# A causal convolution on one core: three row loads of the first loop blocks move into the set-up, and one of the block after them

## The chip, the cores and the metric

The kernel runs on one core of a Trainium2 chip. The metric is the device time of one execution in microseconds; the kernel before takes 733.92 us, the median of three runs (733.46 to 734.03). Lower is better.

## The reference

```python
def setup_inputs():
    B, S, D, K = 8, 4096, 512, 8
    return {
        "x": np.random.randn(B, S, D).astype(np.float32),
        "kernel": np.random.randn(K, D, D).astype(np.float32),
    }

def reference(x, kernel):
    B, S, D = x.shape
    K = kernel.shape[0]
    out = np.zeros_like(x)
    for k in range(K):
        if k == 0:
            shifted = x
        else:
            shifted = np.concatenate([np.zeros((B, k, D), dtype=np.float32), x[:, :-k, :]], axis=1)
        out += np.matmul(shifted, kernel[k])
    return out.astype(np.float32)
```

Each output row is the sum over eight taps `k` of the input row `k` steps earlier (zero before the start of a sequence) times the 512 x 512 matrix of that tap.

## The kernel before

**Layout.** The 8 x 4096 time steps are cut into 128 runs of 256 consecutive steps, one run to a partition. "Row t" is the set of the t-th steps of all 128 runs, a 128 x 512 matrix, so that one row is one matmul operand and the 256 rows are worked through in order. Because a run begins in the middle of a sequence, the rows -7 to -1 are the last rows of the run before, shifted by one partition.

**How a row reaches the matmuls.** The product needs rows with their 512 columns on the partitions, in bf16. From row 12 on this takes two transfers. `load_x(t)` (a DMA on POOL's queue, line 93) casts rows t to t+3 from float32 to bf16 and puts them into a scratch tile `xd` in DRAM; there are enough such tiles that no load waits for a free one. `transpose_x(t)` (a DMA transpose on SP's queue, line 100) then brings these four rows transposed into the ring `XR` of 20 row slots in SBUF, at slot (t + 4) mod 20; it waits for its load and for the last readers of the rows that it overwrites. The set-up also reads rows 0 to 11 directly, transposes them on PE, and loads the eight tap matrices on POOL's queue ahead of everything else.

**The arithmetic.** Rows 0 to 3 are computed by 32 direct products in the set-up. The other 252 rows go in 21 steps of 12 rows. A step saves matmuls by a fast-convolution scheme: it has four nodes, named `PL`, `MI`, `H1` and `H0`, and node k of the list `nodes` (four to a step, from 1) starts at row `n.t` = 4, 16, 28 and so on. Each node forms differences or sums of `XR` rows on DVE (`z`, then `s`, `A` and `F`, line 84), multiplies them by precombined weight matrices on PE (line 125), corrects partial results on DVE and ACT, and is brought out to tiles `y` of a five-buffer pool (`e0`, `e1`, lines 84, 87 and 247). A `PL` node of start t reads rows t-3 to t+7, as does `MI`; `H1` reads t-7 to t-1 and t+1 to t+7; `H0` reads t to t+3 and t+8 to t+11. So the `z` of node 13 (t = 40), for example, reads rows 37 to 47. A store (line 232, SP's queue) writes two output rows from a `y` tile, whose buffer is free again when the store has landed.

**The order.** All order is written by hand: the body is one sequence of calls, each engine takes its own instructions in that order, and each queue its own transfers. The set-up runs the direct products and most of the first step, with parts of the next. Then comes the loop of 21 blocks, called block 0 to block 20 here, over the list `ORDER` of tokens: token `name.i` in block m calls action `name` for node 4m + i + 1, unless `done` says that it was made already. The `AHEAD` table moves calls of the set-up to later nodes. In block 0 much of the list is done already.

**The loads in that order.** The set-up issues the loads of rows 12, 16, 20, 24, 28, 32 and 36 without a wait for compute (POOL reaches the last at 35.88 us). In the loop, actions `r0`, `r1`, `r2` of a node load rows `n.t + 36`, `+40` and `+44`, each made to wait for the DVE instruction that precedes it in the order (`behind`), so that it doesn't run ahead. A block's `ORDER` has three such tokens, `r1.6`, `r2.2` and `r0.2`; in block m they load rows 12m + 56, 12m + 48 and 12m + 40. They are skipped in block 0, and the table `LATE` makes up for it: row 40 is loaded at the end of block 0, and rows 44, 48 and 56 in block 1, beside the regular rows 68, 60 and 52 of that block. The transposes of a block are `x16`, `x20` and, at its end, `x12`: rows 32, 36 and 40 in block 1, rows 44, 48 and 52 in block 2. Rows 24 are transposed twice, in the set-up and in block 0.

POOL also adds pairs of half tiles for the middle output rows (`ga0` to `gb1`, line 276, four to a block from block 1 on). The first of them in each block, at 102.51, 134.78 and 173.38 us in blocks 1, 2 and 3, is used as the mark of the block.

Of the kernel before, what the change touches and what calls it, by code (L numbers as in the profile page):

```python
# [14 lines left out]
def kernel(  # L15
# [79 lines left out]
    def rows(o, t, n):  # L95
        return load(o, xr[:, t:t + n, :])
# [9 lines left out]
    def load_x(t):  # L106
        if t < RUN:
            xd[t] = dpool.tile([P, 4, D], bf, name="xd")
            return rows(xd[t], t, 4)
# [285 lines left out]
    done = set()  # L395

    def do(name, k):
        if k < len(nodes) and (name, k) not in done:
            done.add((name, k))
            ACTS[name](nodes[k])  # L400

    def go(k, name):
        do("a1" if name == "b1" else name, k + AHEAD.get(name, 0))
# [6 lines left out]
    for k in range(7):  # L410
# [184 lines left out]
    go(2, "F0")  # L595
    load_x(32)
    go(4, "l01")
    load_x(36)
    go(4, "l00")
    go(3, "s1")  # L600
    go(4, "b1")
# [10 lines left out]
    go(4, "z")  # L612
    go(4, "A")
    go(4, "g1")
    go(4, "s0")
    go(4, "v0")
    go(4, "d0")
# [2 lines left out]
    go(4, "a1")  # L620
    go(4, "d1")

    done |= {(name, k) for name in ("ga0", "gb0", "ga1", "gb1") for k in (1, 2, 3, 4)}
    done |= {(name, k) for name in ("F0", "F1", "dt", "v0", "v1", "d0", "d1") for k in LEAF}
    LATE = {(0, "d1.4"): [("wl", 8)], (0, "z.6"): [("wh", 8)], (0, "F1.5"): [("r0", 3)],
            (1, "F1.2"): [("r1", 3)], (1, "A.4"): [("r2", 3)], (1, "v1.4"): [("r1", 7)]}
    for m in range(NB):
        for token in ORDER:
            name, i = token.split(".")
            if m or name[0] != "r":  # L630
                do(name, 4 * m + int(i) + 1)
            for late in LATE.get((m, token), ()):
                do(*late)

# [29 lines left out]
```

## Time and profile before

| What | Value |
|---|---|
| median of 3 runs | 733.92 us (733.46 to 734.03) |
| the profiled execution, its own time | 735.01 us |
| its span, first to last instruction | 733.2 us |
| mean granted TensorE clock | 0.993 |
| POOL busy | 142.9 us (19%) |
| ACT busy | 277.3 us (38%) |
| share of the 16 DMA engines: transposes and stores on SP's and ACT's queue (q1) | 48.4% |
| share of the 16 DMA engines: loads on POOL's queue (q0) | 31.1% |
| loads into `xd` | 61 of 512 KB, 7.5 us from issue to landing (median) |
| transposes into `XR` | 62, 5.6 us from issue to landing (median) |
| stores | 127 of 512 KB, 3.5 us from issue to landing (median) |

The span of 733.2 us lies within the profiled execution's own time, with 1.8 us around it; that execution took 1.1 us longer than the median of the runs. Busy time of an engine is the time in which one of its instructions runs; the page also cuts the span into 40 slices of 18.3 us and gives each engine's busy share of every slice in tenths. A row of a timeline has the start, the time taken, the engine, the line, the operation, the tile written and the tiles read, and in brackets how long the engine stood idle just before and what ended that. A transfer has two such times: its issue on POOL's or SP's queue, which is what the timeline shows, and its landing, which the reader of a tile waits for.

### The profile page before, as it was taken

What the parts mean: (1) busy time and instruction counts of PE and PEld (TensorE: products, weight loads), DVE (VectorE), ACT (ScalarE), POOL (GpSimd) and SP (SyncE); (2) the same over time, 40 slices, a digit from 0 to 9 for tenths busy, and PEclk for the clock granted to TensorE, in tenths of its full rate; (3) what the DMA queues carried; (4) which work ended last, traced back from release to release, by engine and by line L of the source; (5) the groups of instructions that cost most, each with busy time, mean ns of one, the idle gap of its engine ahead of it and who ended that gap; (6) DMA issues with size and microseconds to landing.
All of it is one profiled execution on the core that took longest, in us unless ns stands there. A gap on an engine that the chain in (4) does not pass through costs nothing. (4 is left out here: it accounts for less than half of the span.)

```text
span 733.2 us, 8954 instructions
## 1 busy us (share of the span) xinstructions
PE 703.6 (96%) x3205; PEld 315.6 (43%) x3270; DVE 697.4 (95%) x767; ACT 277.3 (38%) x428; POOL 142.9 (19%) x160
## 2 busy tenths in 40 slices
PE   8979989899999999999999999999999999999996
PEld 4434434334444444444444444444444444444442
DVE  1989999799999999999999999999999999999995
ACT  3052433333425253343424335243433524334251
POOL 4200022121131202113121221312112030211202
PEclk9999999989999999999999999999999999999999
DMA  9994699968879796887969788796887979685324
GB/s 200 211 202 126 216 173 242 172 199 180 203 166 222 212 197 189 214 201 169 219 201 187 206 196 204 193 213 195 173 225 176 213 208 182 181 166 180 105 115 172
DMA packets 161451, 139.38 MB, mean 190 GB/s; under 512 B 132224, under 2 KB 136320, under 8 KB 161280
## 3 DMA queue, kind: packets, MB, share of 16 engines
q1 hardware_dynamic: 147536, 100.42, 48.4%
q0 software_dynamic: 13728, 38.15, 31.1%
q8 instruction: 25, 0.41, 0.2%
q10 hardware_dynamic: 144, 0.26, 0.1%
q14 instruction: 18, 0.15, 0.1%
HBM read 77.33 MB, written 99.09 MB: 241 GB/s over the span
## 5 line engine op out<-in xcount | busy, mean ns | idle before, releaser
L125 PE MATMUL pp<-w,F 128*128 128x512 bf16 x1283 | 313.9, 380 | 2.0 <-issue 0.2
L125 PE MATMUL pp<-w,Z 128*128 128x512 bf16 x942 | 232.6, 380 | 2.8 <-DVE Z L84 1.7
L125 PEld LDWEIGHTS <-F 128*128 128x128 bf16 x1312 | 128.5, 98 | 158.8 <-issue 6.7
L276 POOL TENSOR_TENSOR y<-y 128x512 f32<-128x512 f32 x80 | 100.9, 1272 | 429.1 <-DVE Z L84 306.2
L125 PE MATMUL pp<-w,S 128*128 128x512 bf16 x659 | 161.3, 380 | 11.8 <-ACT pp L202 6.6
L84 DVE TENSOR_TENSOR Z<-XR 128x2048 bf16<-128x2048 bf16 (+3 forms) x109 | 154.6, 1437 | 6.7 <-DMA XR<-xd 5.0
L125 PEld LDWEIGHTS <-Z 128*128 128x128 bf16 x960 | 92.4, 98 | 118.2 <-DVE Z L84 12.3
L186 ACT COPY pp<-pp 128x512 f32<-128x512 f32 x82 | 46.7, 570 | 226.6 <-PE pp L125 226.6
L84 DVE TENSOR_TENSOR S<-Z 128x2560 bf16<-128x2560 bf16 x81 | 120.1, 1483 | 0.2 <-remote 0.2
L84 DVE TENSOR_TENSOR F<-S 128x1024 bf16<-128x1024 bf16 x160 | 109.4, 686 | 1.1 <-PE pp L125 0.4
L125 PEld LDWEIGHTS <-S 128*128 128x128 bf16 x672 | 65.6, 98 | 95.0 <-issue 20.4
L204 ACT ACTIVATE pp<-pp 128x512 f32<-128x512 f32 (+1 forms) x84 | 49.1, 585 | 89.2 <-DVE y L87 47.2
L208 ACT COPY DT<-pp 128x512 f32<-128x512 f32 x82 | 48.5, 591 | 59.6 <-PE pp L125 59.6
L93 POOL DMA_DIRECT2D xd<-in_x_dram x61 | 32.4, 531 | 143.7 <-DVE F L84 61.4
L84 DVE TENSOR_TENSOR pp<-DT,pp 128x512 f32<-128x512 f32 x82 | 56.4, 688 | 2.2 <-PE pp L125 2.2
L87 DVE SCALAR_TENSOR_TENSOR pp<-pp,DT 128x512 f32<-128x512 f32 x82 | 56.8, 692 | 0.0
L84 DVE TENSOR_TENSOR Z<-Z 128x1024 bf16<-128x1024 bf16 x78 | 53.6, 687 | 0.6
L84 DVE TENSOR_TENSOR y<-pp,y 128x1024 f32<-128x1024 f32 x42 | 51.2, 1218 | 1.9 <-PE pp L125 1.4
L202 ACT COPY pp<-pp 128x512 f32<-128x512 f32 (+1 forms) x84 | 49.8, 593 | 5.5 <-PE pp L125 5.5
L87 DVE SCALAR_TENSOR_TENSOR y<-pp,y 128x1024 f32<-128x1024 f32 x42 | 51.2, 1218 | 0.3 <-PE pp L125 0.3
L87 DVE SCALAR_TENSOR_TENSOR y<-y,pp 128x1024 f32<-128x1024 f32 (+1 forms) x41 | 48.6, 1187 | 1.8 <-PE pp L125 1.6
L247 ACT COPY y<-pp 128x1024 f32<-128x1024 f32 x40 | 40.7, 1017 | 24.8 <-PE pp L125 23.5
(33 smaller groups left out, 214.3 us busy)
## 6 DMA issues: line engine op xcount, KB each, us to landing
out_dram<-y SPq DMA_DIRECT2D x127, 512.0 KB, 3.5
xd<-in_x_dram POOLq DMA_DIRECT2D x61, 512.0 KB, 7.5
w<-in_kernel_dram POOLq DMA_DIRECT2D x8, 512.0 KB, 15.8
w<-in_x_dram SPq DMA_DIRECT2D x1, 1024.0 KB, 4.9
w<-in_x_dram POOLq DMA_DIRECT2D x2, 512.0 KB, 13.6
XR<-xd SPq DMA_TRANSPOSE x62, 5.6
w<-in_x_dram POOLq DMA_DIRECT2D x2, 256.0 KB, 18.4
w<-in_x_dram POOLq DMA_DIRECT2D x1, 384.0 KB, 20.1
```

The lines of the kernel that those rows point to most:

```text
L84: last["dve"] = nc.vector.tensor_tensor(out=o, in0=a, in1=b, op=op)
L87: last["dve"] = nc.vector.scalar_tensor_tensor(out=o, in0=a, scalar=by, in1=b, op0=MUL, op1=op)
L93: return nc.gpsimd.dma_start(out=o, in_=src)
L125: nc.tensor.matmul(bank, lhsT=comp[:, c * P:(c + 1) * P], rhs=w[:, c, :], start=start and c == 0, stop=c == DC - 1, skip_group_check=True)
L186: nc.scalar.copy(out=n.q[:, 0], in_=n.q[:, 1])
L202: nc.scalar.copy(out=o, in_=q)
L204: nc.scalar.mul(out=o, in_=q, mul=-1.0)
L208: nc.scalar.copy(out=DT, in_=n.q[:, 0])
L247: nc.scalar.copy(out=cc[b_], in_=p)
L276: behind(nc.gpsimd.tensor_tensor(out=cc[b_][:, j], in0=cc[b_][:, j], in1=dd[b_][:, j], op=ADD))
```

## The change

The loads of rows 40, 44 and 48 are issued in the set-up right behind that of row 36, without a wait for compute. The load of row 56 (`r1` of node 7) is issued in the set-up behind `g1`, with its wait for the DVE instruction ahead of it. The entries for the four in `LATE` go. The loop no longer skips the load tokens in block 0: the ones of that block are marked as done, so block 0 issues no load and block 1 its three regular ones, rows 68, 60 and 52.

```diff
     go(2, "F0")
     load_x(32)
     go(4, "l01")
-    load_x(36)
+    for t in range(36, 52, 4):
+        load_x(t)
     go(4, "l00")
...
     go(4, "A")
     go(4, "g1")
+    do("r1", 7)
     go(4, "s0")
...
+    done |= {("r0", 3), ("r1", 3), ("r2", 3)}
     done |= {(name, k) for name in ("ga0", "gb0", "ga1", "gb1") for k in (1, 2, 3, 4)}
     done |= {(name, k) for name in ("F0", "F1", "dt", "v0", "v1", "d0", "d1") for k in LEAF}
-    LATE = {(0, "d1.4"): [("wl", 8)], (0, "z.6"): [("wh", 8)], (0, "F1.5"): [("r0", 3)],
-            (1, "F1.2"): [("r1", 3)], (1, "A.4"): [("r2", 3)], (1, "v1.4"): [("r1", 7)]}
+    LATE = {(0, "d1.4"): [("wl", 8)], (0, "z.6"): [("wh", 8)]}
     for m in range(NB):
         for token in ORDER:
             name, i = token.split(".")
-            if m or name[0] != "r":
-                do(name, 4 * m + int(i) + 1)
+            do(name, 4 * m + int(i) + 1)
```

The functions that it calls are unchanged.

## The prediction

> I write L40 for the load of rows 40 to 43 into DRAM scratch (tile `xd`) and T40 for the transpose of the same rows into the ring `XR`. All times are microseconds of the profiled execution; a median later block is one of those whose first POOL add starts at 173.38 or after.
>
> **What bounds the kernel now.** I read the engine totals first, then the slices, to see whether one engine binds everywhere.
>
> ```profile
> PE 703.6 (96%) x3205; PEld 315.6 (43%) x3270; DVE 697.4 (95%) x767; ACT 277.3 (38%) x428; POOL 142.9 (19%) x160
> ...
> DVE  1989999799999999999999999999999999999995
> ```
>
> PE and DVE are both full nearly throughout, so a transfer matters only where one of them stands still. Apart from the first slices, one DVE digit is low: the eighth, from 128 to 147. Windows as long as a block show what that stretch lost.
>
> ```profile
> 90.50:122.40 31.90, 29.38 (x132) 12.92 (x134) 31.26 (x35) 11.10 (x19) 8.73 (x11) 1.00 0.92 212
> 122.40:154.30 31.90, 26.85 (x113) 11.54 (x113) 25.72 (x28) 10.49 (x16) 5.57 (x5) 0.89 0.83 165
> 154.30:186.20 31.90, 31.44 (x145) 14.18 (x146) 31.21 (x36) 12.63 (x20) 5.37 (x6) 1.00 0.82 198
> 186.20:218.10 31.90, 31.39 (x143) 14.01 (x145) 31.78 (x37) 12.63 (x20) 6.70 (x9) 1.00 0.83 198
> ```
>
> The columns after the length are PE, PEld, DVE, ACT and POOL busy, then the granted clock. DVE has 25.72 where later blocks have 31.8, PE 26.85 for 31.4, and the clock falls to 0.89 there alone. The timeline of that stretch names the wait:
>
> ```profile
> 144.03 2.02 DVE L84 TENSOR_TENSOR Z<-XR 128x3584 bf16<-128x3584 bf16 x1 [5.05 <-DMA XR<-xd]
> ...
> 147.85 1.44 PE L125 MATMUL pp<-w,S 128*128 128x512 bf16 x3 [4.47 <-ACT pp L204]
> ...
> 153.95 1.22 DVE L87 SCALAR_TENSOR_TENSOR y<-y,pp 128x1024 f32<-128x1024 f32 x1 [0.96 <-PE pp L125]
> ...
> 155.69 2.02 DVE L84 TENSOR_TENSOR Z<-XR 128x3584 bf16<-128x3584 bf16 x1 [0.52 <-PE pp L125]
> ```
>
> DVE is ready at 144.03 - 5.05 = 138.98 for the `z` of node 13 (rows 37 to 47) and waits for T44. PE then runs dry for 4.47, and DVE waits for it in turn. The issuing queues show why T44 is late; first SP, then POOL:
>
> ```profile
> 126.80 16.87 SPq L100 DMA_TRANSPOSE XR<-xd  x3
> 147.42 16.30 SPq L232 DMA_DIRECT2D out_dram<-y  x6
> 164.26 10.07 SPq L100 DMA_TRANSPOSE XR<-xd  x3
> ```
>
> ```profile
> 112.71 0.54 POOL L93 DMA_DIRECT2D xd<-in_x_dram  x1 [2.54 <-DVE Z L84]
> 113.95 2.50 POOL L276 TENSOR_TENSOR y<-y 128x512 f32<-128x512 f32 x2 [0.70 <-issue]
> 119.48 1.05 POOL L93 DMA_DIRECT2D xd<-in_x_dram  x2 [3.03 <-DVE Z L84]
> 121.41 0.52 POOL L93 DMA_DIRECT2D xd<-in_x_dram  x1 [0.88 <-DVE pp L84]
> ```
>
> By program order these are L48, then L60 and L56, then L52. The last three are still moving when T40, T44 and T48 are issued from 126.80: the landings in the trace are 127.3, 131.2 and 134.6, T40's 137.4, T44's 143.8. In the next block only two loads (158.01 and 159.94) precede the trio at 164.26, and it is issued in 10.07 instead of 16.87.
>
> **The change, part by part.**
>
> (1) *L44, L48 and L56 leave block 1, L40 leaves block 0.* On POOL that is 4 issues of 0.54, all in POOL's idle time: nothing. On the DMA engines one load costs 2.62: from 40 to 52.5, with loads filling them, the POOL queue moved 2.50 MB of 0.524 MB loads, 4.77 loads in 12.5. Two loads fewer than before (L48 and L56) are in flight in the 8 ahead of T40, so its backlog shrinks by about 5. Block 1 keeps L68, L60 and L52, as every later block has three. So T44 should land as there: 9.4, 10.9, 10.7 and 9.3 after the first transpose of its trio is issued (trios at 164.26, 196.17, 229.01, 292.54), against 17.0 here. DVE wants it 138.98 - 126.80 = 12.2 after: 1.3 to 2.9 of slack, so the wait goes entirely. Two sums of what goes with it:
> - by gaps: 5.05 for `XR`, then 0.17, 0.96 and 0.52 while DVE waits for the slowed PE, and 0.48 at 114.30, where DVE waits for an output tile whose store shared the engines with L44 and L48: 7.18.
> - by block lengths: the first POOL add of blocks 1 to 3 starts at 102.51, 134.78, 173.38, that is 32.27 and 38.60. The block at the same place in the ring comes five later, 31.73 and 31.80. The excess is 0.54 + 6.80 = 7.34, and 0.06 in the block after: 7.40.
>
> I take 7.40; it contains the same gaps and what PE lost between them. What is late next once the wait is gone is DVE itself, 31.8 busy in a block of 31.8.
>
> (2) *L40, L44 and L48 go behind L36 in the set-up.* POOL's issues there wait for the landing of the load eight earlier, so they go out at about 36.9, 39.4 and 41.8, with nothing else on POOL until 85. They are queued on the POOL ring behind L36 and lengthen its busy time by 3 x 2.62 = 7.9. What lies beside it is T12, on SP's ring:
>
> ```profile
> q0 software_dynamic: 690, 2.50, 99.0%
> q1 hardware_dynamic: 484, 0.12, 7.2%
> ...
> 39.47 12.70 SPq L100 DMA_TRANSPOSE XR<-xd  x1
> 52.23 1.14 SPq L232 DMA_DIRECT2D out_dram<-y  x2
> 57.80 4.41 SPq L100 DMA_TRANSPOSE XR<-xd  x2
> ...
> 66.96 1.22 DVE L84 TENSOR_TENSOR Z<-XR 128x2048 bf16<-128x2048 bf16 x1
> ...
> 72.50 2.09 DVE L84 TENSOR_TENSOR Z<-XR 128x1536 bf16<-128x1536 bf16 x2
> ```
>
> While the loads run (first two rows, 40 to 52.5), a transpose gets 7.2% of the engines: 4 KB of a load go by for every 256 bytes. T12 takes 17.0 to land (56.4), and the two stores at 52.23 (57.6 and 58.8), T16 (62.5) and T20 (64.9) stand behind it on SP's ring. All five move back by up to 7.9, less what T12 gets done meanwhile; I take 7.4. Then T12 lands at 63.8 and is wanted at 66.96; the first store at 65.0, its buffer wanted by DVE at 70.23; T16 near 69.5, wanted at 72.50; T20 at 72.3 at the latest, wanted at 73.36 by the second half of the same `z`. The engines stood at 2% from 65 to 72.5, which is the room that this uses. Cost on the path: nothing, with slack of 1.1 to 3. The bounds of the unknown are the price of a load: 2.62 here, and at most 3.9, the spacing of the landings 127.3 and 131.2, where loads met stores and transposes. At 3.9 T20 is 11.7 late, 3.3 over its 8.4 of slack, and the gain is 4.1. I take 2.62, since that row has the same loads beside the same T12. Below nothing there is no room: no wait of DVE in the set-up has one of these loads behind it.
>
> (3) *L56 moves behind the `g1` of the set-up* (DVE, 84.49 to 85.7) and so is issued near 85.8, at POOL's 0.54, with the next POOL work at 102.51. Its 2.62 share the engines with two stores and the repeated T24 (87.89, landing 93.2, wanted by the `z` at 99.95). T24 has 6.8 of slack, the stores' buffers are wanted by ACT at 88.94 (store landed 88.3) and 97.37. In turn L40 no longer meets T32, which took 8.9 to land. Bounds 0 to 1.5: at worst the ACT copy is 2.6 late and PE, which stood 1.68 before 95.76 anyway, covers 1.1. I take 0, since L40 issued at 97.19 moved nothing before 100, so L56 should start near 88.3, as that store ends.
>
> Two rules of the Trainium skill were held against this. "SBUF — State Buffer" (SBUF: two separate sides) says that POOL's DMA descriptors starve while certain DVE operations hold the port they share, about 3.1 instead of 0.62. Here all 61 row loads were issued in 0.52 to 0.55, with DVE busy 95% of the span. By the rule three issues would be 7.4 longer together, which 18 of queued loads would hide, so the sum stays the same. "TensorE: Matmul & The Clock Gate" (Part 1: The HAM clock gate) says that an idle window of about 3.4 halves PE's clock; the 4.47 gap here agrees (clock 0.80 from 140 to 150). By it a shorter stall would cost its own length and no more.
>
> **Sum.** 0 - 7.40 + 0 + 0. Against the profiled execution, 735.01 with a span of 733.2, that gives 727.6 and a span of 725.8. The median of the runs, 733.92, is 1.1 below the profiled one; I take the difference off it: **726.5**.
>
> **Rivals.**
> - *A. The set-up gives part back.* T20 has only about 1 of slack. At 3.9 per load DVE stands 3.3 at the `z` wanting T16 and T20: 733.92 - 4.1 = 729.8. For it: DVE is full there, so any lateness counts. Against: the engines were free for 7.5 ahead of the `z`.
> - *B. Slower.* The same place, deeper: if the POOL ring holds T12 back so long that the lag passes 8.4 + 5.8 = 14.2 (4.7 per load), DVE waits 5.8, and the 1.65 of gaps behind a PE gap as at 147.85 makes 7.4, all of the gain. At 5.6 per load: lag 16.8, stall 8.4 + 1.65 = 10.1, 736.6. Against: the seven loads from L12 to L36 landed at a spacing of 2.5 to 2.7.
> - *C. The wait in block 1 stays in part.* If T44's lateness is due to the stores ahead and not the loads, only one load's worth, 2.6, goes: 2.45 of DVE's wait stay, PE's gap stays short of 4.47 and the 1.65 with it goes: 729.0. Against: later blocks have the same six stores and no wait.
> - *D. It does not do what it says:* the loads leave, T44 comes as late, only the 0.48 goes: 733.4.
>
> **How the numbers follow.** Forecast 0.75 (own range 725.6 to 727.4: 7.18 to 7.40 with the runs' spread of 0.6 and up to 0.8 of stall), A 0.10, B 0.06, C 0.06, D 0.03. The range goes down by the spread to 725.4 and up to A's end, 730.2, which leaves out B, D and a little more. A measurement of this kernel tells about 0.2%, 1.5, from no change: faster 0.91 (forecast, A, C), same 0.03 (D), slower 0.06 (B).
>
> **What would show it.** Step 1: no DVE wait for `XR` near 139, the trio from about 126 issued in 9 to 11, the granted clock 1.00 from 140 to 160, block lengths of 31.7 to 31.9. Step 2: T12 landing about 24 after its issue, loads landing until 63, T20 near 72, and DVE without a gap at 66.96, 70.23 and 72.50. Step 3: no new ACT or PE gap from 88 to 98. I am wrong if DVE waits for `XR` or for a store between 66 and 75, or still waits near 139.

## The result, and the profile after

| What | Before | After |
|---|---|---|
| median of 16 runs each | 733.69 us (728.82 to 735.99) | 728.48 us (727.42 to 730.61) |
| profiled execution, its own time | 735.01 us | 728.58 us |
| its span | 733.2 us | 726.8 us |
| granted clock | 0.993 | 0.997 |

The ratio is 0.9936, with a 95% interval of 0.9918 to 0.9955: faster, by 5.2 us (0.7%) between the medians. The ratios, here and below, are worked out from the fast runs alone and are not quotients of the medians; two slow executions are left out of them (740.88 us in experiment 3, and 928.25 us of the kernel before, beside experiments 6, 8 and 12), while the medians hold them. The spread is a result too: all but three of the 16 runs after lie between 728.2 and 728.8 us, those before over 7 us. The stretch that had stood out, in windows of a block (the columns are as before: PE, PEld, DVE, ACT and POOL busy, then the clock), of the changed kernel:

```profile
90.50:122.40 31.90, 29.77 (x135) 13.26 (x137) 31.74 (x35) 12.17 (x20) 6.59 (x7) 1.00 0.83 195
122.40:154.30 31.90, 31.49 (x144) 14.06 (x146) 31.77 (x35) 12.62 (x20) 6.68 (x8) 1.00 0.85 198
```

DVE has 31.77 where it had 25.72, and the clock stays at 1.00. On SP's queue the trio of transposes at the end of block 1 is as short as the later ones (9.66 for 16.87):

```profile
127.32 9.66 SPq L100 DMA_TRANSPOSE XR<-xd  x3
142.99 14.46 SPq L232 DMA_DIRECT2D out_dram<-y  x6
157.98 10.62 SPq L100 DMA_TRANSPOSE XR<-xd  x3
```

POOL, and then DVE, around it:

```profile
120.00 0.54 POOL L93 DMA_DIRECT2D xd<-in_x_dram  x1 [2.46 <-DVE Z L84]
121.93 0.52 POOL L93 DMA_DIRECT2D xd<-in_x_dram  x1 [1.39 <-DVE pp L84]
135.30 1.27 POOL L276 TENSOR_TENSOR y<-y 128x512 f32<-128x512 f32 x1 [12.86 <-DVE Z L84]
136.60 0.54 POOL L93 DMA_DIRECT2D xd<-in_x_dram  x1
```

```profile
138.02 1.48 DVE L84 TENSOR_TENSOR S<-Z 128x2560 bf16<-128x2560 bf16 x1
139.59 2.02 DVE L84 TENSOR_TENSOR Z<-XR 128x3584 bf16<-128x3584 bf16 x1
```

Two loads (L60, L52) precede the trio, T44 lands at 137.35, and the `z` of node 13 starts with no bracket: no wait. The load at 136.60 is L80, of the next block; it matters below. In the set-up, SP's queue shows what the moved loads cost:

```profile
39.97 20.46 SPq L100 DMA_TRANSPOSE XR<-xd  x1
60.50 1.20 SPq L232 DMA_DIRECT2D out_dram<-y  x2
61.81 7.25 SPq L100 DMA_TRANSPOSE XR<-xd  x2
```

T12 takes 20.46 to be issued instead of 12.70. It lands at 64.74, T16 at 69.66, T20 at 71.76; DVE wants them at 68.07, 73.60 and 74.47 and has no gap there.

### The profile page after: what moved, and what is told of

Same layout as the page of the kernel before. It is cut to its first block, busy times and chain, and to the rows that moved or that the text cites. A ratio compares the mean times of both kernels' runs of the same rounds, so it can differ in the third digit from the quotient of the medians.

```text
span 726.8 us, 8952 instructions
## 1 busy us (share of the span) xinstructions
PE 701.1 (96%) x3205; PEld 314.9 (43%) x3270; DVE 696.9 (96%) x767; ACT 277.3 (38%) x428; POOL 142.7 (20%) x160
```

## The experiments

All times are medians, beside the kernel before on the same chip (733.07 to 733.50). The places named are those of the listing.

**1. The kernel before, profiled again.** No edit.

> The kernel before, once more, for a second profile of it. Theory (the wait for the transposes of rows 40 and 44 at the end of block 1 is a race between transfers, so its length differs from run to run): times between 729 and 736 us, and the profile shows a DVE wait for XR near 139 us of another length than 5.05 us; the first weights land at 11.2 or at 12.3 us, whichever way that start fell. Rival (the wait is a fixed 5.05 us, and the spread of the times comes from elsewhere): the same wait within 0.3 us, whatever the time.

Median 733.28 us over 12 runs (728.18 to 735.05). The profiled one took 729.28 us, and its `z` of node 13 reads

```profile
140.30 2.02 DVE L84 TENSOR_TENSOR Z<-XR 128x3584 bf16<-128x3584 bf16 x1 [0.68 <-PE pp L125]
```

T44 landed at 140.10 (the bracket names PE, but DVE starts 0.2 after that landing), where the first profile had 143.84. The same program waits 0.68 us in one execution and 5.05 us in another. Blocks 1 and 2 took 33.09 and 32.31 us, 1.9 over the usual, not 7.4; most of the 1.9 is a wait of 1.30 at 114.93 for an output tile whose store was late (0.48 at 114.30 in the first profile). The two executions differ by 5.73 us in their times, and these two blocks (5.5) and the landing of the first weights (10.95 for 11.19) make up the whole of it. So the length of the wait is not fixed: the same transfers, issued in the same order, end in one way or the other. I call that a race.

**2. Load 56 alone moved; 3. load 56 alone left in block 1.**

```diff
# 2: the kernel before
     go(4, "g1")
+    do("r1", 7)
...
-            ..., (1, "v1.4"): [("r1", 7)]}
# 3: the changed kernel
-    do("r1", 7)
...
+            ..., (1, "v1.4"): [("r1", 7)]}
```

> The kernel before with the load of row 56 alone moved to the set-up; rows 40, 44 and 48 stay in the loop. Theory (every load that is queued in the 8 us ahead of the trio of transposes holds it up by its own 2.6 to 3.9 us): the DVE wait near 139 us shrinks from 5.05 to between 1.2 and 2.5 us, block 1 to block 2 takes 33 to 34.5 us, time 729.5 to 731 us. Rival (the stores ahead of the transposes are the cause): wait 4.5 to 5 us, time about 733.5 us.

> The changed kernel with the load of row 56 left in block 1 where it was; rows 40, 44 and 48 in the set-up. Theory: one load of 2.6 to 3.9 us more ahead of the trio than in the changed kernel, where row 44 landed 2.2 us ahead of DVE: a wait of 0.4 to 1.7 us comes back, time 729 to 730.5 us. Rival (the early loads of rows 40 to 48 did all of it): no wait, 728.5 us.

(2) 729.26 us, ratio 0.9940 (0.9925 to 0.9956): in its profile T44 lands at 138.71, and the `z` of node 13 has no wait:

```profile
140.03 2.03 DVE L84 TENSOR_TENSOR Z<-XR 128x3584 bf16<-128x3584 bf16 x1
```

What DVE waits for there is 0.27 for `XR` at 106.94, and 1.36 at 115.26 for a store that met L44 and T36 (landing at 112.11 and 113.76). (3) 733.36 us, ratio 0.9984 (0.9965 to 1.0003), no better than before, with

```profile
143.61 2.03 DVE L84 TENSOR_TENSOR Z<-XR 128x3584 bf16<-128x3584 bf16 x1 [5.00 <-DMA XR<-xd]
```

So it is L56 that counts: with it gone the wait is gone, with it back the whole wait is back, although L40, L44 and L48 have left the loop. L48 had landed at 120.24 in the kernel before, 6.6 us ahead of the trio; its leaving wins nothing at the `z`. Ahead of the trio stand L60, L56 and L52 in the kernel before and in (3), L60 and L52 in the changed kernel and in (2). Waits that add up load by load, as I had it, give 1.2 to 2.5 us in (2) and 0.4 to 1.7 in (3): both missed. One load makes the difference between no wait and 5 us, which is more than its own 2.6 to 3.9.

**4. A load that nobody reads.** The changed kernel, with rows loaded a second time at the place of L56.

```diff
+    def again(t):
+        behind(rows(dpool.tile([P, 4, D], bf, name="xd"), t, 4))
...
+            (1, "v1.4"): [("xx", 9)]}
```

> The changed kernel with one load of four rows made once more in block 1, at the place where the load of row 56 stood, into a scratch tile that nobody reads. Theory (traffic alone does it: one load more ahead of the trio is enough to lose the race against the load of row 80): as with row 56 left there, median about 733 us, spread 729 to 735. Rival (it is rows 40 to 56 themselves coming late, or POOL's order): no wait, 728.5 us.

733.88 us, ratio 1.0009 (0.9989 to 1.0029): the gain is gone. T44 landed at 143.34, and DVE waited:

```profile
143.53 2.03 DVE L84 TENSOR_TENSOR Z<-XR 128x3584 bf16<-128x3584 bf16 x1 [5.14 <-DMA XR<-xd]
```

Traffic alone does it; which rows come late is no matter.

**5. Load 80 held back.** The kernel before, with the first load of block 2 behind the `z` of node 13.

```diff
+            ..., (2, "v0.3"): [("r1", 15)]}
...
-            if m or name[0] != "r":
+            if (m or name[0] != "r") and (m, token) != (2, "r1.6"):
```

> The kernel before with one edit: in block 2 the load of row 80 is issued not right behind the first POOL add (136 us) but after the z of node 13, behind v0.3; rows 40 to 56 stay where they were. Theory (a race: the transposes of rows 40 and 44 come late by the loads ahead, and it is the load of row 80, whose 4 KB packets reach the engines at about 138.5 us, that holds up the last packets of row 44 until 143): the DVE wait near 139 us falls from 5 us to below 0.8 us in every run, time 728.5 to 730 us with a small spread. Rival (the loads ahead alone make the wait, as I predicted it): no change, 733 us with the spread of before.

729.16 us (727.55 to 730.84), ratio 0.9961 (0.9941 to 0.9982), with all of L40, L44, L48 and L56 where they were. The wait of its `z` is a little over the 0.8 that was expected at most:

```profile
139.17 2.02 DVE L84 TENSOR_TENSOR Z<-XR 128x3584 bf16<-128x3584 bf16 x1 [0.89 <-DMA XR<-xd]
```

The queues from 138.5 to 143 us in experiment 4, where L80 was issued at 135.49 (columns: packets, MB, share of the 16 engines; q1 is SP's, q0 POOL's):

```profile
q1 hardware_dynamic: 556, 0.14, 71.0%
q0 software_dynamic: 103, 0.36, 46.2%
```

and in this one, where L80 is issued at 142.48:

```profile
q1 hardware_dynamic: 1837, 0.46, 49.8%
```

Without L80 the transposes move 1837 packets in these 4.5 us, with it 556 (920 in the profile of experiment 1, where L80 is there too). In the kernel before, L80 is the second row of POOL in block 2:

```profile
134.78 1.27 POOL L276 TENSOR_TENSOR y<-y 128x512 f32<-128x512 f32 x1 [12.86 <-DVE Z L84]
136.08 0.54 POOL L93 DMA_DIRECT2D xd<-in_x_dram  x1
```

Its first packet moves at 138.6, 2.5 us after the issue; in experiment 4 at 137.7, in the changed kernel at 138.5. The reading is: if T44 is through by then (137.35 in the changed kernel), nothing happens; if much of it is left, the remainder is held up by L80 and lands with it: 143.84 and 143.93 in the kernel before, 143.34 and 143.23 in experiment 4. The line is not sharp: in experiment 1 L80's first packet moved at 138.6 too, and T44 landed 1.5 us later, at 140.10. The loads ahead decide whether the race is lost; L80 sets how much that costs.

**6. Both: the unread load, and load 80 held back.** The edits of 4 and 5 on the changed kernel.

> The changed kernel with the repeated load in block 1 (which took it back to 733.9 us) and, besides, the load of row 80 moved behind the z of node 13. Theory (the repeated load alone makes row 44 late by 0 to 1 us, and the load of row 80 makes 5 us of it): a wait below 1 us near 139 us, 728 to 729.5 us. Rival (the repeated load is what costs): 733 us as without the second edit.

729.15 us, ratio 0.9951 (0.9934 to 0.9968), against 733.88 without the second edit. The profiled wait was 2.44 us and not below 1, so the loads ahead alone can still cost that much; the median is in the range.

```profile
140.88 2.03 DVE L84 TENSOR_TENSOR Z<-XR 128x3584 bf16<-128x3584 bf16 x1 [2.44 <-DMA XR<-xd]
```

Set side by side, the profiles split the wait into its two parts. T44 lands after the first transpose of its trio is issued, by the number of loads issued in the 8 us ahead of that (DVE asks for it at about 12.2):

| Loads ahead | T44 lands after | Where |
|---|---|---|
| none, one | 7.5, 7.6 us | experiments 11, 10 |
| two | 10.0 to 11.0 us | the changed kernel, 2, 7, 8, 9, 12 |
| three, L80 held back | 12.9, 14.4 us | 5, 6 |
| three, L80 in its place | 12.7, and 17.0 to 17.1 us | 1, and before, 3, 4 |

The third load brings T44 over the limit by 0.5 to 2.2 us; L80 adds up to about 4 us more, or, as in experiment 1, nothing that shows.

**7. The three loads at 77 us, 8. at 62 us, 9. at 59 us.** The changed kernel, with the loads behind a DVE instruction.

```diff
# 7; in 8 and 9 they wait for a DVE instruction noted earlier, behind go(2, "s") or wsum(MI, LO, MID)
-    for t in range(36, 52, 4):
-        load_x(t)
+    load_x(36)
+    do("r0", 3)
+    do("r1", 3)
+    do("r2", 3)
```

> The changed kernel with the loads of rows 40, 44 and 48 not in the first stretch, where they hold up the transposes of rows 12 to 20, but behind the DVE instruction at about 77 us, where the DMA engines are half idle. Theory (the set-up hides those three loads in full): 728.5 us, within 0.5 us, with row 20 landed at about 65 to 66 us instead of 71.8. Rival (the three loads cost something in the set-up, which is why the time came out at 728.5 and not 726.5): 726.5 to 727.5 us.

> The changed kernel with the loads of rows 40, 44 and 48 made to wait for the DVE instruction at 62 us, so that they move between 65 and 73 us, where the DMA engines stood at 2% in the kernel before: behind the transposes of rows 12 to 20 and ahead of that of row 24. Theory (it is a question of which transfer on SP's queue they meet, and there they meet none): row 20 lands at 65 us, no DVE wait, the time of the changed kernel within 0.5 us. Rival (any later place than the first stretch costs, as 77 us did): 731 us and more.

> As the kernel with the three loads at 62 us, but waiting for the DVE instruction that ends at about 59 us, so that they are through before the store of 72.6 us and before the transpose of row 24. They share the engines with the transposes of rows 16 and 20: row 20 lands at 68 to 72 us, wanted at 73.4. Theory A (with nothing moved ahead of 55 us the first weights land at 11.0 to 11.2 us, as in all six profiles without loads added there, and no transfer is waited for): span 725.6 to 725.9, time 727.3 to 727.7 us, 1 us below the changed kernel. Theory B (the start varies by itself): median 728.3 to 728.7 us, as the changed kernel.

(7) 736.77 us, ratio 1.0045 (1.0028 to 1.0062): slower than before, against both guesses. SP's queue, then POOL's, then DVE in its profile:

```profile
77.77 9.28 SPq L100 DMA_TRANSPOSE XR<-xd  x1
87.15 3.05 SPq L232 DMA_DIRECT2D out_dram<-y  x3
98.88 12.25 SPq L100 DMA_TRANSPOSE XR<-xd  x4
```

```profile
77.61 1.55 POOL L93 DMA_DIRECT2D xd<-in_x_dram  x3 [41.32 <-DVE y L84]
```

```profile
106.54 1.23 DVE L84 TENSOR_TENSOR Z<-XR 128x2048 bf16<-128x2048 bf16 x1 [6.64 <-DMA XR<-xd]
```

T24, issued at 77.77, met these loads and L56 behind them and landed 21.1 us later; the second T24 waits for the first, T28 and T32 stand behind both on SP's queue, and DVE is out of rows for 6.64 us. (8) 728.42 us, ratio 0.9950 (0.9931 to 0.9968), as the changed kernel, though not quite without a wait: DVE stands 0.65 for a store that was issued at 72.6 and met the last load. (9) 729.97 us, ratio 0.9967 (0.9946 to 0.9988): four us earlier the loads meet T16 and T20. T20 lands at 74.58, and DVE waits 1.29 for it, and 1.30 for PE at 101.51. Neither theory of (9) held, since both had T20 in time. In these four places it is the transpose that the loads meet there, and its slack, that decides whether the place is free, and not how busy the DMA engines are on average.

**10. One load more in the first stretch, 11. three more.** `range(36, 52, 4)` becomes `range(36, 56, 4)` and `range(36, 64, 4)`; the loads go from where they stood.

> The changed kernel with the load of row 52 also issued in the set-up, right behind row 48: four loads more than before instead of three. The transpose of row 20 landed at 71.8 us in the changed kernel and DVE wants it at 74.5: one load of 2.65 us uses that up. Theory (the set-up's cover is what the slack says): row 20 at 74.4, a DVE wait of 0 to 0.6 us there, time 728.3 to 729.2 us. Rival (the cover is already used up): 730 us and more.

> The changed kernel with rows 52, 56 and 60 also issued in the set-up behind row 48: six loads more there than before. Theory (the slack of 2.7 us is all the cover there is): row 12 lands near 72.7 and DVE waits for it 4.5 us at 68 us, row 20 near 79.7 for another 0.7, with 1.7 us for the slowed PE behind it: 733.7 to 735.5 us, slower than the kernel before. Rival (the set-up hides loads without limit): 728.5 us.

(10) 730.35 us, ratio 0.9966 (0.9944 to 0.9987), where its rival stands, with T20 at 75.08 for the 74.4 expected, and

```profile
75.17 1.23 DVE L84 TENSOR_TENSOR Z<-XR 128x2048 bf16<-128x2048 bf16 x1 [1.70 <-DMA XR<-xd]
```

(11) 735.36 us, ratio 1.0053 (1.0033 to 1.0073), slower than before, with

```profile
72.12 1.23 DVE L84 TENSOR_TENSOR Z<-XR 128x2048 bf16<-128x2048 bf16 x1 [3.99 <-DMA XR<-xd]
...
80.48 1.23 DVE L84 TENSOR_TENSOR Z<-XR 128x2048 bf16<-128x2048 bf16 x1 [1.88 <-DMA XR<-xd]
```

The first wait is for T12, the second for T20. It is the kind of lag that rival B names, but B put its wait at T16 and T20 alone and had it come from dearer loads; here it comes from more of them, landing 2.6 to 2.8 us apart. The first stretch takes three and is used up with the fourth.

**12. The changed kernel again.**

> The changed kernel once more, beside the next two. In its first profile the first weights landed 1.1 us later than in the kernel before (12.3 instead of 11.2 us), ahead of anything that the change touches. Theory (that start is not set by the change): span 725.7 us where the start is the early one, 726.7 where it is late, with no DVE wait for a transfer behind 20 us in either; median between 727.5 and 728.5 us. Rival (the change itself costs the 1.1 us): every run at 728.3 to 728.8 us, with the late start.

728.64 us (727.58 to 728.81), ratio 0.9944 (0.9922 to 0.9966). The first weights landed at 11.74 us and the span was 726.3; in its first profile it was 12.30 and 726.8. So span less start is 714.5 and 714.6, and the start varies: no fixed cost of the change, though its median lay above the range. All seven profiles with loads added to the first stretch, the two of the changed kernel among them, had that start between 11.05 and 12.30 us, the other seven between 10.72 and 11.19. The loads are issued 25 us later, and I know no way in which they could act on it; whether it is chance stays open.

No version beat the changed kernel clearly: the one with the loads at 62 us (728.42) is its equal, and the kernel before with load 80 held back alone (729.16), or with load 56 alone moved (729.26), comes within 0.8 us of it.

## Why the prediction came out as it did

**The stretch and the direction were right.** L56 no longer stands ahead of the trio, T44 lands 10.0 us after the first transpose of its trio is issued (9.3 to 10.9 forecast), DVE's wait near 139 goes, the clock stays at 1.00, blocks 1 and 2 take 31.70 and 31.80 us. The time, 728.48, is in the range, 2.0 above the forecast.

**The term that was mis-sized is the 7.40 of the sum, and with it "I take the difference off it".** 7.40 was the loss of one execution of 735.01 us. That execution stood 1.1 above the median, and the reading that fits is that it had lost more than the usual: another profile of the same kernel lost 1.9, 5.5 less, and its time was 5.73 lower (experiment 1). Taking the median's 733.92 and all of 7.40 off it counts the 1.1 twice. Against the execution's own time the sum gave 727.6, and the changed kernel's profile came to 728.58 with its first weights 1.1 us later: 727.5 with the same start.

**The mechanism of step 1 was half of it.** "Its backlog shrinks by about 5" counts two loads at 2.62, L48 and L56. Experiment 3 shows that L48's part is nothing: T44 lands 17.0 after its trio's issue with L48 gone, as before. L56 alone is worth about 2 to 4 us there (the table behind experiment 6), and the rest, up to about 4 us, is L80's, whose packets meet T44 only when it is late. L80 was in the timeline of before, issued at 136.08 and landing at 143.93, within 0.1 us of T44, and I did not list it among what T44 met. That the wait goes entirely came out right by the other way that I took it, from the landings of later blocks, which have two loads ahead; that the two loads' 5 and the measured drop of 7.0 (17.0 to 10.0) lie near each other is luck. Rival C priced what is left of the wait without L80 too. L40, L44 and L48 bring, as far as the medians show, the 0.8 us between experiment 2 and the changed kernel; the wait for a store at 115 that is gone with them (0.48, 1.30 and 1.36 in three profiles, none in that of experiment 5) would fit.

**Step 2 was right, its slack too.** Forecast for T12, T16 and T20: 63.8, 69.5, at most 72.3; measured 64.74, 69.66 and 71.76, the whole schedule 1.1 late. T20 had 2.7 of slack where I put 1.1 or more, and a fourth load costs DVE 1.70, as the closeness suggested. Rivals A and B did not happen in this change; more loads made waits of their kind in experiments 10 and 11.

**Step 3 was right on the path, tighter than I had it.** L56, issued at 87.10, kept the repeated T24 9.5 us from issue to landing (5.3 before): at 98.52 it had 2.5 us left before the `z` at 101.05, not 6.8. No new gap of ACT or PE came from 88 to 98.

## What to carry to other kernels

Before a transfer's lateness is costed, list every transfer that shares its time on the engines, those that are issued after it too: a late transpose can lose more to the load that comes next than to the ones that made it late. A wait in one profile is one draw; where transfers race, a second profile of the same kernel tells its size better than a sum. A move of loads is free only as long as the transposes that they meet at the new place have slack for it, and in-order queues pass the delay on to what stands behind.

## What was not expected of the hardware

A transpose beside loads is held up more than the loads are: from 40 to 52.5 us of the kernel before it moved 0.12 MB while the loads moved 2.50 MB, and in experiment 7 one took 21.1 us to land, against a median of 5.6. In the kernel before, the outcome of one such meeting goes with a spread of 7 us in the time.
